# Merge stage regrouped into two seven-product blocks beside three chunks each, with X+Z on VectorE and whole attention outputs in DRAM

## The chip, the cores and the metric

The kernel runs on one core of a Trainium2 chip, in fp32 throughout. The metric is the device time of one execution in microseconds. Before the change the median of three runs is 2468.08 us (2466.44 to 2469.51). The core's engines are TensorE (matrix products), VectorE, ScalarE, GpSimd (POOL) and SyncE (SP); the last two and ScalarE also issue DMAs.

## The reference

Two layers of a decoder trunk, on 256 positions of width 2048. Each layer normalises x, projects it to ten segments, runs two attentions side by side, gates both, projects each, merges them by sigmoid gates and adds an output projection to x.

```python
h = rms_norm(x, norm_gain)
proj = jnp.einsum('bsd,de->bse', h, w_in)
(da_q, da_k, da_v, da_z, sb_q, sb_k, sb_v, sb_z, gate_a, gate_b) = split_columns(proj)
...
ua = oa.reshape(b, s, DA_WIDTH) * jax.nn.silu(da_z)          # differential attention, 8 heads
ub = stick_breaking_attention(qs, ks, vs) * jax.nn.silu(sb_z) # 16 heads
y = (jax.nn.sigmoid(gate_a) * jnp.einsum('bse,ed->bsd', ua, w_branch_a)
     + jax.nn.sigmoid(gate_b) * jnp.einsum('bse,ed->bsd', ub, w_branch_b))
return x + jnp.einsum('bsd,de->bse', y, w_out)
```

Each of the ten segments, the two branch projections and the output projection is a product of 256 x 2048 by 2048 x 2048. The weights are far larger than the core's memory and are streamed once per layer.

## The kernel before, in words

**Splitting.** Each fp32 operand is split into a high part in TensorE's fast fp32 format and the remainder (`split`, L63: a ScalarE copy to `wh`, L64, and a VectorE subtraction to `wl`, L65). A product is three matmuls, high by high, high by low, low by high (`mm3`, L67 to L71). Weights come by DMA into tiles `raw` of 128 x 1024 (512 KB: two slices of 128 rows by 512 columns), loaded on SyncE's queue (`load_raw`, L86 to L88) into a pool of 11 buffers, and are split as soon as they are there.

**A chunk** (`c_stream`, L102) is 512 output columns for all 256 positions: eight steps, each one raw tile and 2 x 2 x 3 = 12 matmuls of 512 columns, into two banks named `mc` (or `sU` and `sN`, with `alt`). After the last step a function `fin` reads the banks; `gap` adds two empty steps, in which the chunk does nothing.

**A block** (`s_stream`, L127) is two chunks at once by a seven-product scheme of Strassen's kind, on 2 x 2 quarters: on the left positions by depth, on the right depth by the two chunks. The weights' quarters are b11, b21, b12 and b22, four raw tiles each. The left sums `sm` (tiles `smh`, `sml`) are made once per layer. The right sums are made in the raw tiles. `add_dma` (L145 to L147) adds a quarter from DRAM to a raw tile by an accumulating DMA on GpSimd's queue, `add` (L149 to L151) adds one raw tile to another on VectorE. The products, four steps each, every step a split and six matmuls, are in order:

| product | right operand | then | bank |
|---|---|---|---|
| first U | X = b11 | X += b12 by DMA | sU, copied to p1 |
| N | Z = b22 | Z += b12 by DMA | sN |
| Q | X | X += b22 by DMA | sQ, copied to p5 (L190) |
| second U | X | | sU, on top; w = U - p5 on VectorE (L195), results with N |
| V | Z | | sQ |
| R | W = b21 | X += W on VectorE (L209) | sN, result with p1 |
| last V | X | | sQ, on top, result with u |

X's four raw tiles are held for the whole block, Z's from N to V.

**The interleave.** `run` (L222) advances several streams by their share of steps done: with weights n, always the stream with the smallest (steps done + 0.5) / n. A block counts 28 steps and a chunk 10 with its gap. So program order mixes block steps and chunk steps; a scheduler then orders each engine's instructions by that order, with weight splits and right sums ahead by a priority offset.

**Stages of a layer.** Differential attention in four groups, all by chunks (L683 to L695); each group's output goes through `da_out` (L577), which transposes it on TensorE, splits it and spills both parts to DRAM by GpSimd DMAs (`spill`, L495). Then four stick-breaking groups (L707 to L733): scores (`sb_weights`), then the block for V and Z beside two chunks, the next group's Q and K; in the fourth group the two chunks are gates a0 and a1. `sb_out` (L626) multiplies, splits and spills. The merge (L778 to L789): a0 and a1 beside the block of gates a2 and a3; a2 and a3 beside the block of gates b0 and b1; then all of ub is reloaded (L782) by GpSimd DMAs, the block of gates b2 and b3 takes nine steps alone, and its rest runs beside b0 (L783 to L786); b1 to b3 follow as plain chunks, and the output projection as four more. `reload` (L699) puts the parts of a group into the tiles listed in `GZ_TAGS`; ub's tiles are those that ua held. Sigmoids of gates and the a-branch products go to DRAM (`sig_d`, `ya_d`) and come back by SyncE (`back`, L738).

**The start.** `first_input` (L333) loads x transposed in pieces of two slices, makes the high part on ScalarE (L339) and the low on VectorE (L340), ahead of the first chunk's weights step by step.

Of the kernel before, what the change touches and what calls it, by code (L numbers as in the profile page):

```python
# [9 lines left out]
F32 = mybir.dt.float32  # L10
# [23 lines left out]
RAW = 11  # L34
# [7 lines left out]
def trunk(ctx: ExitStack, tc: tile.TileContext, x, xT, gT, norm_gain, w_in, qk_gain, lam_vecs,  # L42
# [42 lines left out]

    def load_raw(src):  # L86
        raw = raw_tile()
        nc.sync.dma_start(out=raw, in_=src)  # L88
        return raw
# [7 lines left out]

    def at_k(x, k):

        return x[k // 4][:, k % 4] if isinstance(x, list) else x[:, k]  # L100

    def c_stream(src, lhs, fin, alt=False, gap=0, before=None):  # L102
# [5 lines left out]
        for kp in range(KP):  # L108
            if before is not None:
                before(kp)  # L110
            h, l = split_raw(load_raw(src[kp]))
            order = [(kk, t) for kk in range(KK) for t in range(NT)]
            if kp == KP - 1:
                order.sort(key=lambda o: o[1])
            for kk, t in order:
# [3 lines left out]
                    k == 0, k == KT - 1)  # L119
            if kp < KP - 1:  # L120
                yield
# [5 lines left out]
    def s_stream(sl, sr, xh, sm, fin):  # L127
# [45 lines left out]
        def held(nm):  # L173
            return wp.tile([P, CW], F32, name="pp", bufs=PPB)

# [14 lines left out]
        nc.scalar.copy(p5, q_ps)  # L190
        yield

# [12 lines left out]
        yield  # L205
# [118 lines left out]
    ident = const.tile([P, P], F32, name="ident")  # L324
    make_identity(nc, ident)
    mhalf = const.tile([P, 4], F32, name="mhalf")
    nc.gpsimd.memset(mhalf, -0.5)

# [4 lines left out]
    def first_input(kp):  # L333
        raw = tok()
        nc.sync.dma_start(out=raw, in_=xT[:, kp * CW:(kp + 1) * CW])
        for j in range(KK):
            k = kp * KK + j
            rv = raw[:, j * S:(j + 1) * S]
            nc.scalar.mul(xr[0][:, k], rv, gcol[:, k:k + 1])  # L339
# [5 lines left out]
    def sums_of_squares():  # L345
        for c in range(NG):
            for t in range(NT):
# [6 lines left out]
                     before=first_input)))  # L354
# [15 lines left out]
    for l in range(DEPTH):  # L370
# [42 lines left out]
        u_dram = {b: [dram.tile([P, KT, S], F32R, name=f"u{b}{p}") for p in "hl"] for b in "ab"}  # L413
# [3 lines left out]
        def da_fin(nm, g):  # L417

            def fin(ps):
# [4 lines left out]
                for t in range(NT):  # L424
                    ns.append(work.tile([P, CW], F32, name="ev", bufs=2))
# [65 lines left out]
        def u_stage():  # L491
# [85 lines left out]
        def da_out(g, aT, v, gz):  # L577
# [19 lines left out]
            us = u_stage()  # L597
            for t in range(NT):
                u = tok()
                nc.vector.tensor_tensor(out=u, in0=hold[:, t], in1=gz[:, t], op=ALU.mult)  # L600
                put_T(u, us, 0, t)
# [24 lines left out]
        def sb_out(g, wT, v, gzT):  # L626
            us = u_stage()
            for hp in range(0, HPG, 2):
# [10 lines left out]
                u = tok()  # L639
                uv = u.rearrange("p (h q) -> p h q", q=S)  # L640
                nc.vector.tensor_tensor(out=uv, in0=ov, in1=gzT[:, hp:hp + 2], op=ALU.mult)
                split(us[0][:, hp:hp + 2], us[1][:, hp:hp + 2], uv)
# [63 lines left out]
        ua, ub = ([], []), ([], [])  # L706
        for g in range(NG):  # L707
# [7 lines left out]
            def z_T():  # L715
                gzT.append(att.tile([P, HPG, S], F32, name="gzT", tag="hold"))
                for t in range(NT):
                    tr = ps_at.tile([P, CW], F32, name="at")
                    for h in range(HPG):
# [6 lines left out]
                         lambda col, t, op: (fv, fz)[col](t, op))  # L726
            if g + 1 < NG:
                c = chain(q_stream(NG + g + 1, xt, False, GAP), k_stream(NG + g + 1, xt, False, GAP))
# [153 lines left out]
```

## Time and profile before

| | |
|---|---|
| median of the runs | 2468.08 us |
| the profiled execution's own time | 2464.42 us |
| its span, first to last instruction | 2462.7 us |
| TensorE's mean granted clock | 0.988 |
| TensorE, VectorE, ScalarE, GpSimd busy | 97%, 71%, 62%, 16% |
| moved by DMA | 571.21 MB |

In a table by stretches, each engine has its busy microseconds and (x) its number of instructions in the stretch; then come the granted clock of TensorE (1.00 is full), the mean busy share of the 16 DMA engines, and GB/s. A matmul's recorded time overlaps with the next one's, so that a run of them is read from their starts or their count, and not from durations. A row of waits has who waited for whom, the sum of microseconds, how often, and the longest. A row of groups has, behind the names and shapes, the count, then the busy sum and the mean in ns, then the idle time of the engine ahead of it with what ended that. A row of the timeline has start, duration, engine, line and names, and in brackets the idle time before it. A row of DMAs ends with the size and the median time from issue to landing.

### The profile page before, as it was taken

Reading aid. Unit: us, or ns where it says so; the run is one execution under the profiler, and the core shown is the slowest. Engines: PE = TensorE matmul, PEld = TensorE weight load, DVE = VectorE, ACT = ScalarE, POOL = GpSimd, SP = SyncE. Lnnn points to the kernel's source line nnn. Section 1 sums busy time; section 2 is a strip of 40 time slices with the busy share of each in tenths; the row PEclk is TensorE's granted clock in tenths of the full one; section 3 lists DMA queues with packets and bytes.
Section 4 is the critical chain, followed back from the end, with each engine's and each line's share of the span. In section 5 each row is a group of like instructions: output and inputs, shape, how many; then the busy total and the mean of one; then the engine's idle time right before and its main releaser. Section 6 shows DMA issues by size and latency. Waiting matters only on the chain.

```text
span 2462.7 us, 31649 instructions
## 1 busy us (share of the span) xinstructions
PE 2384.9 (97%) x10996; PEld 1965.0 (80%) x10996; DVE 1743.6 (71%) x1979; ACT 1531.9 (62%) x2214; POOL 393.7 (16%) x476
## 2 busy tenths in 40 slices
PE   8999999999999999899999999999999998997999
PEld 6888888788887777688888888887888877876887
DVE  5677767688787676575666776777887876766754
ACT  6666666677777555454565676667777775655543
POOL 1132230200101211200020321302101112112000
PEclk9999999999999999899999999999999999999999
DMA  9546646888988989987665465378889889899873
GB/s 338 174 141 225 197 137 232 210 239 229 247 239 246 296 266 274 293 315 250 212 207 180 151 221 187 119 249 208 247 238 229 247 248 295 281 289 264 320 233 102
DMA packets 163040, 571.21 MB, mean 232 GB/s; under 512 B 18624, under 2 KB 19136, under 8 KB 162880
## 3 DMA queue, kind: packets, MB, share of 16 engines
q1 hardware_dynamic: 120960, 423.55, 50.8%
q0 software_dynamic: 39328, 141.58, 24.9%
q10 hardware_dynamic: 2592, 4.07, 0.5%
q8 instruction: 86, 1.41, 0.2%
q14 instruction: 74, 0.61, 0.1%
HBM read 535.57 MB, written 33.55 MB: 231 GB/s over the span
## 4 chain that ended last, share of the span: by engine, by line
PE 67%; issue 17%; DMA 7%; POOL 4%; DVE 2%; ACT 2%; POOLq 0%; SPq 0%; ACTq 0%; DVEq 0%
PE mc L69 11%; PE mc L70 11%; PE mc L71 11%; DMA raw<-in_w_in 6%; PE sU L70 4%; PE sN L70 4%; PE sU L71 4%; PE sN L71 4%; PE sN L69 4%; PE sU L69 4%; POOL raw L147 2%; PE at L243 2%; PE sQ L70 1%; PE sQ L69 1%; PE sQ L71 1%
## 5 line engine op out<-in xcount | busy, mean ns | idle before, releaser
L65 DVE TENSOR_TENSOR wl<-raw,wh 128x1024 fp32r<-128x1024 f32 x1000 | 1209.8, 1222 | 495.3 <-PE mc L70 158.9
L64 ACT CAST wh<-raw 128x1024 fp32r<-128x1024 f32 x1000 | 1045.9, 1053 | 724.4 <-PE mc L71 280.9
L147 POOL DMA_DIRECT2D raw<-in_w_in x168 | 145.5, 868 | 743.0 <-DVE wl L65 466.3
L70 PE MATMUL mc<-wl,xTh 128*128 128x512 f32 x576 | 225.9, 392 | 0.4 <-DVE wl L65 0.2
L71 PE MATMUL mc<-wh,xTl 128*128 128x512 f32 x576 | 225.0, 391 | 0.0
L69 PE MATMUL mc<-wh,xTh 128*128 128x512 f32 x576 | 207.0, 394 | 5.5 <-ACT tok L465 3.4
L69 PE MATMUL mc<-wh,xrh 128*128 128x512 f32 x512 | 198.6, 392 | 8.6 <-ACT wh L64 8.5
L70 PE MATMUL mc<-wl,xrh 128*128 128x512 f32 x512 | 201.8, 394 | 1.8 <-DVE wl L65 1.8
L71 PE MATMUL mc<-wh,xrl 128*128 128x512 f32 x512 | 200.9, 392 | 0.0
L69 PEld LDWEIGHTS mc<-wh,xTh 128*128 128x128 f32 x576 | 107.8, 189 | 29.9 <-ACT wh L64 4.3
L70 PEld LDWEIGHTS mc<-wl,xTh 128*128 128x128 f32 x576 | 108.5, 188 | 25.6 <-DVE wl L65 3.5
L71 PEld LDWEIGHTS mc<-wh,xTl 128*128 128x128 f32 x576 | 108.5, 188 | 21.7
L69 PEld LDWEIGHTS mc<-wh,xrh 128*128 128x128 f32 x512 | 96.4, 189 | 29.3 <-ACT wh L64 9.5
L70 PEld LDWEIGHTS mc<-wl,xrh 128*128 128x128 f32 x512 | 96.6, 189 | 23.3 <-DVE wl L65 3.7
L71 PEld LDWEIGHTS mc<-wh,xrl 128*128 128x128 f32 x512 | 96.6, 189 | 19.2
L252 POOL TENSOR_SCALAR rv<-ssq 128x4 f32<-128x4 f32 (+1 forms) x48 | 40.2, 837 | 419.4 <-ACT junk L433 379.4
L70 PE MATMUL sU<-wl,xrh 128*128 128x512 f32 x256 | 100.6, 393 | 1.1 <-DVE wl L65 1.1
L71 PE MATMUL sN<-wh,xrl 128*128 128x512 f32 x256 | 100.5, 393 | 0.0
L70 PE MATMUL mc<-wl,ua 128*128 128x512 f32 x256 | 100.2, 391 | 0.2 <-DVE wl L65 0.2
L71 PE MATMUL sU<-wh,xrl 128*128 128x512 f32 x256 | 100.2, 391 | 0.0
L69 PE MATMUL sN<-wh,xrh 128*128 128x512 f32 x256 | 100.1, 391 | 0.0
L70 PE MATMUL sN<-wl,xrh 128*128 128x512 f32 x256 | 99.9, 390 | 0.0
(258 smaller groups left out, 5010.6 us busy)
## 6 DMA issues: line engine op xcount, KB each, us to landing
raw<-in_w_in SPq DMA_DIRECT2D x584, 512.0 KB, 4.4
raw<-in_w_in POOLq DMA_DIRECT2D x168, 512.0 KB, 9.7
raw<-in_w_a SPq DMA_DIRECT2D x64, 512.0 KB, 5.7
raw<-in_w_b SPq DMA_DIRECT2D x64, 512.0 KB, 5.8
raw<-in_w_o SPq DMA_DIRECT2D x64, 512.0 KB, 4.3
uah<-uh POOLq DMA_DIRECT2D x8, 512.0 KB, 4.9
ual<-ul POOLq DMA_DIRECT2D x8, 512.0 KB, 6.9
ubh<-uh POOLq DMA_DIRECT2D x8, 512.0 KB, 6.4
```

Source lines behind the costliest of these rows:

```text
L64: nc.scalar.copy(h, src)
L65: nc.vector.tensor_tensor(out=l, in0=src, in1=h.bitcast(F32), op=ALU.subtract)
L69: nc.tensor.matmul(ps, lhsT=lh, rhs=rh, start=start, stop=False, **kw)
L70: nc.tensor.matmul(ps, lhsT=lh, rhs=rl, start=False, stop=False, **kw)
L71: nc.tensor.matmul(ps, lhsT=ll, rhs=rh, start=False, stop=stop, **kw)
L147: nc.gpsimd.dma_start(out=dst, in_=src, accum_op=ALU.add)
L243: nc.tensor.transpose(out=tr[:, j * P:(j + 1) * P], in_=src[:, j * P:(j + 1) * P], identity=ident)
L252: nc.gpsimd.tensor_scalar(out=v[:, :w], in0=ss, scalar1=1.0 / n, scalar2=RMS_EPS, op0=ALU.mult, op1=ALU.add)
```

## The change

Blocks get a switch `tb_dma`. With it (stick-breaking groups one to three), Z takes b12 after N and X takes b22 after Q, both by DMA as before, but V comes between Q and the second U. Without it (group four and the merge's blocks), Z stays b22 through N; after each of Q's steps VectorE adds Z to X, and Z then takes b12 by DMA; V stays behind U.

Group four runs its block beside three chunks (gates a0, a1 and b0). The merge has two blocks: gates a2 and a3 beside a0, a1 and the chunk of gate b1; gates b2 and b3 beside a2, a3, the reload of ub and b0. Gates b0 and b1 are so two chunks instead of a block. The attention outputs are spilled as one fp32 tile, loaded back through SyncE's queue into raw tiles and split then. The last stick-breaking group is neither spilled nor reloaded, and the b-branch chunks take its depth first. The raw pool has 12 buffers; the two `ev` buffers are taken from the pool of `pp`. At the start the first weights come and are split in two halves, the first piece of x comes in two, and its high part is made on VectorE. A first copy of two constants, made twice before, goes.

```diff
-RAW = 11
+RAW = 12
...
+    def first_slice(src, between):
+        raw = raw_tile()
+        h = wp.tile([P, KK * CW], F32R, name="wh", bufs=4)
+        l = wp.tile([P, KK * CW], F32R, name="wl")
+        for i in range(KK):
+            c = slice(i * CW, (i + 1) * CW)
+            nc.sync.dma_start(out=raw[:, c], in_=src[:, c])
+            if i == 0:
+                between()
+            with tc.high_priority(offset=400):
+                split(h[:, c], l[:, c], raw[:, c])
+        return h, l
...
-        yield from prod(n_ps, s(3), loader(zs, b22), lambda i: add_dma(zs[i], b12[i]))
+        yield from prod(n_ps, s(3), loader(zs, b22),
+                        (lambda i: add_dma(zs[i], b12[i])) if tb_dma else None)
         yield
+        def next_sums(i):
+            if tb_dma:
+                add_dma(xs[i], b22[i])
+            else:
+                add(xs[i], zs[i])
+                add_dma(zs[i], b12[i])
         q_ps = ps_s.tile([P, CW], F32, name="sQ")
-        yield from prod(q_ps, s(0), lambda i: xs[i], lambda i: add_dma(xs[i], b22[i]))
+        yield from prod(q_ps, s(0), lambda i: xs[i], next_sums)
         p5 = held("p5")
         nc.scalar.copy(p5, q_ps)
         yield
+        if tb_dma:
+            v_ps = ps_s.tile([P, CW], F32, name="sQ")
+            yield from prod(v_ps, s(2), lambda i: zs[i], None, False)
+            yield
         yield from prod(u_ps, s(1), lambda i: xs[i], None, True)
...
-        v_ps = ps_s.tile([P, CW], F32, name="sQ")
-        yield from prod(v_ps, s(2), lambda i: zs[i], None, False)
+        if not tb_dma:
+            v_ps = ps_s.tile([P, CW], F32, name="sQ")
+            yield from prod(v_ps, s(2), lambda i: zs[i], None, False)
...
+            else:
+                nc.sync.dma_start(out=rv, in_=xT[:, k * S:(k + 1) * S])
+                nc.vector.tensor_scalar(out=xr[0][:, k], in0=rv, scalar1=gcol[:, k:k + 1],
+                                        scalar2=None, op0=ALU.mult)
...
-                    ns.append(work.tile([P, CW], F32, name="ev", bufs=2))
+                    ns.append(held("ev"))
...
         def spill(b, g, u):
-            for i in range(2):
-                nc.gpsimd.dma_start(out=u_dram[b][i][:, g * 4:(g + 1) * 4], in_=u[i])
+            nc.gpsimd.dma_start(out=u_dram[b][:, g * 4:(g + 1) * 4], in_=u)
...
         def reload(b, groups, u):
             for g in groups:
+                raw = load_raw(u_dram[b][:, g * 4:(g + 1) * 4].rearrange("p h s -> p (h s)"))
+                ts = [att.tile([P, 4, S], F32R, name="u" + b, tag=tag) for tag in GZ_TAGS[g]]
+                split(ts[0], ts[1], raw.rearrange("p (h s) -> p h s", s=S))
                 for i in range(2):
-                    ut = att.tile([P, 4, S], F32R, name="u" + b, tag=GZ_TAGS[g][i])
-                    nc.gpsimd.dma_start(out=ut, in_=u_dram[b][i][:, g * 4:(g + 1) * 4])
-                    u[i].append(ut)
+                    u[i][g] = ts[i]
...
-                c = chain(c_stream(w_chunk(GATE_A, 0), xt, sig_fin("a", 0), False, GAP),
-                          c_stream(w_chunk(GATE_A, 1), xt, sig_fin("a", 1), False, GAP))
-            run((2 * (C_STEPS + GAP), c), (S_STEPS, s))
-            sb_out(g, wT, v, gzT[0])
+                c = [gate_chunk("a", 0), gate_chunk("a", 1), gate_chunk("b", 0)]
+            run((len(c) * (C_STEPS + GAP), chain(*c)), (S_STEPS, s))
+            last_u = sb_out(g, wT, v, gzT[0])
...
-            return c_stream([w_b[l, c, kp] for kp in range(KP)], ub, fin, alt, gap, before)
+            return c_stream([w_b[l, c, kp] for kp in range(KP)], ub, fin, alt, gap, before,
+                            depth=[KP - 2, KP - 1, *range(KP - 2)])
...
-        run((2 * (C_STEPS + GAP), chain(a_stream(0, False, GAP), a_stream(1, False, GAP))),
-            (S_STEPS, gate_block("a", 2)))
-        run((2 * (C_STEPS + GAP), chain(a_stream(2, False, GAP), a_stream(3, False, GAP))),
-            (S_STEPS, gate_block("b", 0)))
-        reload("b", range(NG), ub)
-        late = gate_block("b", 2)
-        for _ in range(S_STEPS // 3):
-            next(late)
-        run((C_STEPS + GAP, b_stream(0, False, GAP)), (S_STEPS - S_STEPS // 3, late))
+        def back_ub():
+            reload("b", range(NG - 1), ub)
+            yield
+        c = [a_stream(0, False, GAP), a_stream(1, False, GAP), gate_chunk("b", 1)]
+        run((len(c) * (C_STEPS + GAP), chain(*c)), (S_STEPS, gate_block("a", 2)))
+        c = [a_stream(2, False, GAP), a_stream(3, False, GAP), back_ub(), b_stream(0, False, GAP)]
+        run((3 * (C_STEPS + GAP), chain(*c)), (S_STEPS, gate_block("b", 2)))
         run((1, b_stream(1)))
```

More of the change, by code (lines that the diff above doesn't have):

```diff
@@ L84, in raw_tile, with held @@
         return wp.tile([P, KK * CW], F32, name="raw", bufs=RAW)
+    def held(nm):
+        return wp.tile([P, CW], F32, name="pp", bufs=PPB)
     def load_raw(src):
@@ L96, in split_raw, with c_stream @@
         return h, l
+    def first_slice(src, between):
[10 more added lines that the diff above has]
+        return h, l
     def at_k(x, k):
         return x[k // 4][:, k % 4] if isinstance(x, list) else x[:, k]
-    def c_stream(src, lhs, fin, alt=False, gap=0, before=None):
+    def c_stream(src, lhs, fin, alt=False, gap=0, before=None, first=False, depth=range(KP)):
         if alt:
@@ L107, in c_stream @@
             ps = [ps_c.tile([P, CW], F32, name="mc") for _ in range(NT)]
[L108 to L111, printed above, removed]
+        for i, kp in enumerate(depth):
+            if first and i == 0:
+                h, l = first_slice(src[kp], lambda: before(0))
+            else:
+                if before is not None:
+                    before(i)
+                h, l = split_raw(load_raw(src[kp]))
             order = [(kk, t) for kk in range(KK) for t in range(NT)]
-            if kp == KP - 1:
+            if i == KP - 1:
                 order.sort(key=lambda o: o[1])
@@ L118, in c_stream @@
                 mm3(ps[t], at_k(lhs[0], k)[:, ts], at_k(lhs[1], k)[:, ts], h[:, cs], l[:, cs],
-                    k == 0, k == KT - 1)
-            if kp < KP - 1:
+                    i + kk == 0, i == KP - 1 and kk == KK - 1)
+            if i < KP - 1:
                 yield
@@ L125, in c_stream, with s_stream @@
             yield
-    def s_stream(sl, sr, xh, sm, fin):
+    def s_stream(sl, sr, xh, sm, fin, tb_dma=False):
         hk = KP // 2
@@ L199, in s_stream @@
         yield
-        v_ps = ps_s.tile([P, CW], F32, name="sQ")
-        yield from prod(v_ps, s(2), lambda i: zs[i], None, False)
+        if not tb_dma:
+            v_ps = ps_s.tile([P, CW], F32, name="sQ")
+            yield from prod(v_ps, s(2), lambda i: zs[i], None, False)
         fin(1, 1, lambda dst: nc.vector.scalar_tensor_tensor(
             out=dst, in0=v_ps, scalar=-1.0, in1=w, op0=ALU.mult, op1=ALU.subtract))
-        yield
+        if not tb_dma:
+            yield
         def add_w(i):
@@ L334, in first_input @@
         raw = tok()
-        nc.sync.dma_start(out=raw, in_=xT[:, kp * CW:(kp + 1) * CW])
+        if kp:
+            nc.sync.dma_start(out=raw, in_=xT[:, kp * CW:(kp + 1) * CW])
         for j in range(KK):
@@ L338, in first_input @@
             rv = raw[:, j * S:(j + 1) * S]
-            nc.scalar.mul(xr[0][:, k], rv, gcol[:, k:k + 1])
+            if kp:
+                nc.scalar.mul(xr[0][:, k], rv, gcol[:, k:k + 1])
+            else:
+                nc.sync.dma_start(out=rv, in_=xT[:, k * S:(k + 1) * S])
+                nc.vector.tensor_scalar(out=xr[0][:, k], in0=rv, scalar1=gcol[:, k:k + 1],
+                                        scalar2=None, op0=ALU.mult)
             nc.vector.scalar_tensor_tensor(out=xr[1][:, k], in0=rv, scalar=gcol[:, k:k + 1],
@@ L353, in trunk @@
     run((1, c_stream([w_in[0, DA_Q, kp] for kp in range(KP)], xr, lambda ps: first.update(ps=ps),
-                     before=first_input)))
+                     before=first_input, first=True)))
     sums_of_squares()
@@ L600, in da_out @@
                 nc.vector.tensor_tensor(out=u, in0=hold[:, t], in1=gz[:, t], op=ALU.mult)
-                put_T(u, us, 0, t)
+                tr = ps_at.tile([P, CW], F32, name="at")
+                for j in range(HPG):
+                    nc.tensor.transpose(out=tr[:, j * P:(j + 1) * P], in_=u[:, j * P:(j + 1) * P],
+                                        identity=ident)
+                nc.scalar.copy(us[:, :, t * P:(t + 1) * P], heads(tr))
             spill("a", g, us)
@@ L626, in sb_out @@
         def sb_out(g, wT, v, gzT):
-            us = u_stage()
+            keep = g == NG - 1
+            if keep:
+                uh, ul = u_parts()
+            else:
+                us = att.tile([P, HPG, S], F32, name="us", tag="aTh")
             for hp in range(0, HPG, 2):
@@ L638, in sb_out @@
                         False, True)
[L639 to L642, printed above, removed]
+                hs = slice(hp, hp + 2)
+                uv = tok().rearrange("p (h q) -> p h q", q=S) if keep else us[:, hs]
+                nc.vector.tensor_tensor(out=uv, in0=ov, in1=gzT[:, hs], op=ALU.mult)
+                if keep:
+                    split(uh[:, hs], ul[:, hs], uv)
+            if keep:
+                return uh, ul
             spill("b", g, us)
```

24 lines of the change are left out of this document (12 added, 12 removed).

## The prediction, made blind

> **What bounds the kernel now.** I read the page's first part, then busy time by stretches cut at the stages, TensorE's waits, and the timeline around the longest wait.
>
> ```profile
> span 2462.7 us, 31649 instructions
> PE 2384.9 (97%) x10996; PEld 1965.0 (80%) x10996; DVE 1743.6 (71%) x1979; ACT 1531.9 (62%) x2214; POOL 393.7 (16%) x476
> ```
> ```profile
> core 0: us, PE busy (x) PEld busy (x) DVE busy (x) ACT busy (x) POOL busy (x), PEclk, DMA share, GB/s
> 0.00:60.00 60.00, 49.54 (x202) 38.81 (x203) 33.07 (x47) 39.67 (x76) 7.38 (x22) 1.00 0.90 339
> 60.00:466.00 406.00, 405.44 (x1941) 338.62 (x1940) 290.64 (x395) 265.60 (x514) 91.59 (x90) 1.00 0.58 187
> 466.00:745.00 279.00, 275.17 (x1324) 227.85 (x1324) 226.54 (x245) 201.41 (x248) 33.95 (x42) 1.00 0.86 235
> 745.00:1065.00 320.00, 294.15 (x1253) 237.59 (x1252) 219.94 (x206) 186.99 (x201) 57.73 (x81) 0.94 0.94 277
> 1065.00:1690.00 625.00, 624.43 (x2937) 519.73 (x2936) 427.37 (x539) 379.22 (x658) 107.66 (x114) 1.00 0.64 207
> 1690.00:1965.00 275.00, 271.68 (x1311) 225.42 (x1310) 222.07 (x242) 198.10 (x245) 32.51 (x40) 1.00 0.86 237
> 1965.00:2285.00 320.00, 291.42 (x1261) 234.48 (x1260) 220.84 (x208) 188.14 (x202) 58.31 (x82) 0.96 0.94 277
> 2285.00:2463.00 178.00, 173.10 (x778) 142.49 (x776) 103.18 (x104) 72.76 (x75) 4.53 (x7) 1.00 0.63 212
> ```
> TensorE is the bound, and where it idles is plain. Through 60–466 and 1065–1690 (differential attention, then output and the next layer) it idles 0.6 us each. In the first three stick-breaking groups it idles 3.8 and 3.3 us by layer. In the fourth group and the merge it idles 25.9 and 28.6 us, and there the clock is below 1. Per layer that clock is worth 0.06 × 320 = 19.2 and 0.04 × 320 = 12.8 us. Idle and clock in these four stretches make 61.6 + 32.0 = **93.6 us**; all else is matmul at full pace, except the start.
>
> ```profile
> 2390.00:2430.00 40.00, 40.00 (x178) 33.11 (x177) 20.96 (x19) 15.86 (x15) 0.00 (x0) 1.00 0.63 197
> ```
> This stretch holds only 512-column matmuls of the output projection. They overlap, so their price is the spacing: 40 / 178 = 0.225, or 0.227 without the two that straddle the edges. A block step (6 matmuls) takes 1.36 us, a chunk step (12) 2.72 us.
>
> ```profile
> PE sU L69 <- ACT wh L64: 44.0, 11, 9.7
> PE mc L69 <- ACT wh L64: 11.9, 11, 7.5
> PE sU L70 <- DVE wl L65: 6.2, 12, 0.8
> PE mc L69 <- ACT tok L465: 3.4, 2, 1.7
> PE sQ L69 <- ACT wh L64: 2.9, 2, 1.5
> ```
> ```profile
> 859.33 0.39 PE L69 MATMUL sQ<-wh,smh 128*128 128x512 f32 x1
> 866.89 0.79 PE L69 MATMUL sU<-wh,smh 128*128 128x512 f32 x1 [7.17 <-ACT wh L64]
> 867.48 0.63 PE L70 MATMUL sQ<-wl,smh 128*128 128x512 f32 x1
> 867.91 0.63 PE L71 MATMUL sQ<-wh,sml 128*128 128x512 f32 x1
> ...
> 871.32 0.63 PE L71 MATMUL sU<-wh,sml 128*128 128x512 f32 x1
> ```
> ```profile
> 865.79 1.05 ACT L64 CAST wh<-raw 128x1024 fp32r<-128x1024 f32 x1 [10.64 <-DMA raw<-in_w_in]
> ```
> ```profile
> L147 POOL DMA_DIRECT2D raw<-in_w_in x168: 841/861/1152, 435.2 to 2247.4; - x168
>   ACT wh L64: 115.8, 45
> DMA to landing us min/median/max: 5.1/9.7/20.9
> ```
> So nearly all idle time precedes one product: U's second half (sU from the left sums), straight after Q. Its operand is X with b22 added by the accumulating DMA, issued when Q has read X; ScalarE waited for such landings 115.8 us in all. I worked out the interleave of `run` by hand: from Q's first step to U's first lie four block steps and only two chunk steps, because the chunk is then in its two empty steps: 4 × 1.36 + 2 × 2.72 = 10.9 us. A landing takes 9.7 us at the median and 20.9 at worst. That decides it. After the stop the matmuls come 0.43 us apart (867.48 to 867.91), about half pace, until 871.32 and a little on: some 5 us, of which 5 × (1 − 0.227 / 0.43) = 2.4 us are lost.
>
> **The change, part by part.**
>
> *Order.* In the three blocks per layer with accumulated Z (`tb_dma`), V now lies between Q and U. By the same rule from Q0 to U0 there are eight block and four chunk steps: 21.8 us, over the worst landing. In the other three (group four, gates a2–3, b2–3) VectorE makes X+Z, so U waits for no DMA; Z takes b12 by DMA after that, and until V come eight block and eight chunk steps: 32.6 us. The Q-to-U wait goes everywhere. Late next would be X's first accumulation, wanted by Q (8 × 1.36 + 6 × 2.72 = 27 us after U's first step), which is unchanged and late only in the block that today starts with nine steps alone; no block starts alone now. So I remove the 93.6 us and add back what is left.
>
> *Matmuls.* Gates b0 and b1 turn from a block (7 × 24 = 168 matmuls) into two chunks (2 × 96 = 192). 24 more per layer: 48 × 0.227 = **+10.9 us**, on the path.
>
> *Traffic.*
> ```profile
> raw<-in_w_in SPq DMA_DIRECT2D x584, 512.0 KB, 4.4
> ua<-uah POOLq DMA_DIRECT2D x8, 512.0 KB, 8.1
> ```
> Per layer the accumulating DMAs fall from 7 × 12 = 84 to 3 × 12 + 3 × 8 = 60, the block-to-chunk swap adds 4 plain loads, spills fall from 16 to 7 and reloads from 16 to 7: 38 transfers of 512 KB fewer. In group four and merge, weights and reloads were 4 × 24 + 7 × 8 + 16 = 168 transfers and become 3 × 20 + 9 × 8 + 7 = 139. At 277 GB/s before, over a stretch about as long, that is some 230 GB/s, what the earlier groups moved (235) with 1% idle. The new reloads go through SP's queue among the weights (4.4 us each) instead of POOL's (8.1); the three of b stand ahead of b0's own weights, but b0 begins with the group that stayed in SBUF.
>
> *VectorE and ScalarE.*
> ```profile
> L65 DVE TENSOR_TENSOR wl<-raw,wh 128x1024 fp32r<-128x1024 f32 x1000 | 1209.8, 1222 | 495.3 <-PE mc L70 158.9
> L64 ACT CAST wh<-raw 128x1024 fp32r<-128x1024 f32 x1000 | 1045.9, 1053 | 724.4 <-PE mc L71 280.9
> L151 DVE TENSOR_TENSOR raw<-raw 128x1024 f32<-128x1024 f32 x56 | 68.5, 1223 | 24.4 <-DMA raw<-in_w_in 24.1
> L190 ACT COPY pp<-sQ 128x512 f32<-128x512 f32 x14 | 8.1, 578 | 1.8 <-PE sQ L71 1.8
> ```
> Per layer the swap drops 12 splits and 4 additions, the reloads add 7 splits, X+Z adds 12 additions: VectorE +3 × 1.22 us, less 14 half-size low parts that the unsplit spills don't need: about nothing. In a three-chunk stage it has 52 splits and 8 additions, 60 × 1.22 = 73 us, plus some 10 of small work, in 3 × 21.8 + 38.1 = 103.5 us: covered on average. During Q it has 2.45 us a step, and two of those steps have no chunk beside them. R does the same today (split and addition in L209) and shows up in no wait, so between 0 and 1.6 us each I take 0.5: 6 × 0.5 = **+3 us**. If the cover were gone, each of the 24 X+Z additions would cost its 1.22, 29 us.
>
> *A new wait.* V uses the bank sQ that Q just filled, with only an empty chunk step between, so its first matmul waits for the copy p5. Queued behind it on TensorE are V's other matmuls and the next chunk's; ScalarE and VectorE, which wait for those to free the split buffers, stop with it. Bounds: 0, if a chunk's matmul is placed between; 0.39 + 0.58 plus one split ahead on ScalarE (1.05), 2.0 us, at most. The nearest row is the wait for L465, 1.7 us, also a bank held by a ScalarE copy, and only in 2 blocks of 14. I take 1.0: 6 × 1.0 = **+6 us**. The L465 waits stay: **+3.4**.
>
> ```profile
> 760.00:780.00 20.00, 16.56 (x57) 12.15 (x56) 11.21 (x12) 18.23 (x21) 5.00 (x8) 0.74 0.90 266
> 953.00:959.00 6.00, 4.74 (x13) 3.50 (x14) 3.05 (x3) 2.13 (x3) 0.57 (x1) 0.72 1.07 223
> ```
> Such waits keep their bare length only if they stay short. The 1.7 us ones above lie in a stretch at 1.00, but 1.3 us idle in 953–959 already goes with 0.72. I count clock only from there on. The Trainium skill ("TensorE: Matmul & The Clock Gate", Part 1) says that the clock halves after an idle window of about 3.4 us; the trace agrees for the 7.2 us wait and not for 953–959, where less idle time was enough. By the rule alone every remaining wait would cost its length.
>
> *Start.*
> ```profile
> 4.87 0.91 ACT L339 ACTIVATE xrh<-tok,gcol 128x256 fp32r<-128x256 f32 x2 [2.86 <-DMA gcol<-in_gT]
> 6.36 1.05 ACT L64 CAST wh<-raw 128x1024 fp32r<-128x1024 f32 x1 [0.59 <-DMA raw<-in_w_in]
> 7.46 1.22 PE L69 MATMUL mc<-wh,xrh 128*128 128x512 f32 x2 [7.46 <-ACT wh L64]
> ```
> Half of the first weights is loaded and split alone, and VectorE makes xr: the split shrinks by about 0.5 us, and the half load lands earlier. But 339 GB/s runs through these 60 us, so an earlier start can run into later loads. Between 0 and −2.5: **−1.2 us**.
>
> Free: the retained group of b, the one-copy spill (its work lies beside 70–90% busy engines that TensorE doesn't wait for), the shared ring for `ev`, the dropped constants, the twelfth raw buffer.
>
> **Sum**: 2462.7 − 93.6 + 10.9 + 3 + 6 + 3.4 − 1.2 = 2391.2 us span. The profiled execution took 2464.42, 1.7 more than its span, and lies 3.7 under the median of the runs: 2391.2 + 1.7 + 3.7 = **2397 us**.
>
> **Rivals.**
>
> *Slower: bandwidth, not order.* The stretches with the waits have DMA share 0.94. If the landings stretch with the engines' load whatever the order, X+Z and V only move the wait to the weights of the three chunks, and the added matmuls remain: 2468 + 10.9 − 1.2 = 2478. It decides if the share stays at 0.94 and Z's accumulation takes over 32 us in the merge. For it: the one long landing, 20.9 us. Against it: 339 GB/s at the start and the 29 transfers fewer. The change then doesn't do what its order is for.
>
> *V behind p5 is dear.* 2.0 us and half pace after it (2.4) in each of six blocks: 6 × 4.4 = 26 instead of 6, 2417. By the skill's rule, waits of 2.0 us keep the clock: 12 instead of 6, 2403.
>
> *The raw ring chokes at b's reload.* Its three raw tiles wait for a3 to free the tiles of ua, beside X's four and Z's last two: 9 of 12 held, 3 left for loads. A stop like today's longest, 9.7 + 2.4 us, in each layer: +24, 2421. Against: b's splits come as soon as a3 has passed each group.
>
> **Chances.** Forecast with its own range of 2380 to 2410: 0.66. Dear V, choked ring, or VectorE short in Q: 0.21, to 2440. Slower by bandwidth: 0.06. About no change, part of each: 0.03. Everything hidden and the start at its best, 2376 to 2380: 0.04. The range, 2378 to 2435, leaves out the last three and the tail. Runs of before spread by 3 us, so 0.2% (5 us) is what can be told: faster 0.91, same 0.03, slower 0.06.
>
> **What would show it.** Right: TensorE's waits for sU gone from 44 to under 8; the clock 0.99 or more in group four and merge; DMA share there near 0.87; x11044 matmuls; 120 accumulating DMAs; first matmul near 6. Wrong: sU or mc still waiting for ScalarE's split behind DMA landings (bandwidth); new waits of sQ for L190's copy over 10 us; a stop near b0; VectorE's split ending TensorE's waits in Q.

## The result, and the profile after

The changed kernel takes 2406.65 us (median of 4 runs, 2406.20 to 2407.71), beside 2467.26 for the kernel before: ratio 0.9756, interval 0.9739 to 0.9773. It is 2.4% faster; the prediction was 2397 us with a range of 2378 to 2435. The experiments below show that this is not the change's own grouping at work: of its two large parts, one alone (the order of the products) gives 2398, and a third arrangement 2386.

The page's first lines:

```profile
span 2404.2 us, 31450 instructions
PE 2373.1 (99%) x11044; PEld 1966.8 (82%) x11044; DVE 1735.8 (72%) x1950; ACT 1508.3 (63%) x2181; POOL 322.0 (13%) x375
```

There are 48 matmuls more, as counted beforehand, in a span that is 58.5 us shorter. The stretches of the stick-breaking groups and the merge (idle of TensorE is the stretch less PE busy):

```profile
core 0: us, PE busy (x) PEld busy (x) DVE busy (x) ACT busy (x) POOL busy (x), PEclk, DMA share, GB/s
466.00:745.00 279.00, 277.62 (x1349) 232.17 (x1348) 226.97 (x244) 203.84 (x249) 30.75 (x37) 1.00 0.85 234
745.00:1050.00 305.00, 296.65 (x1315) 243.35 (x1314) 229.68 (x211) 184.51 (x195) 31.43 (x45) 0.99 0.82 254
1690.00:1950.00 260.00, 259.31 (x1265) 217.18 (x1264) 211.53 (x225) 188.24 (x228) 25.45 (x31) 1.00 0.81 225
1950.00:2230.00 280.00, 274.26 (x1216) 224.53 (x1216) 214.03 (x197) 170.50 (x179) 29.62 (x42) 1.00 0.83 254
```

Idle is 1.4 + 8.4 + 0.7 + 5.7 = 16.2 us where it was 61.6, and the clock, worth 32 us before, is worth 0.01 × 305 = 3. TensorE's waits, the longest in total:

```profile
PE mc L70 <- DVE wl L65: 9.6, 10, 3.7
PE sQ L70 <- DVE wl L65: 7.1, 10, 1.0
PE mc L69 <- DVE xrh L371: 5.3, 1, 5.3
PE mc L69 <- ACT wh L64: 3.5, 5, 2.3
PE sQ L69 <- ACT pp L216: 1.0, 2, 0.5
```

The row that led before, sU with 44.0 us, is gone. ScalarE's waits for landings tell the same; the first row is of the kernel before, the second of the changed one (longest wait at the end of the row):

```profile
ACT wh L64 <- DMA raw<-in_w_in: 127.1, 53, 13.1
```
```profile
ACT wh L64 <- DMA raw<-in_w_in: 15.4, 7, 4.2
```

And the accumulating DMAs themselves land sooner at worst (median 9.7 and worst 20.9 before):

```profile
L167 POOL DMA_DIRECT2D raw<-in_w_in x120: 838/858/1225, 437.3 to 2179.0; - x120
DMA to landing us min/median/max: 5.2/8.0/9.8
```

Where is the rest? The largest single wait that is left lies around b0's first steps. TensorE, SyncE and VectorE there:

```profile
1014.67 0.40 PE L71 MATMUL sQ<-wh,sml 128*128 128x512 f32 x1
1018.72 0.79 PE L70 MATMUL mc<-wl,uh 128*128 128x512 f32 x1 [3.65 <-DVE wl L65]
1019.31 0.63 PE L71 MATMUL mc<-wh,ul 128*128 128x512 f32 x1
1019.74 0.63 PE L70 MATMUL mc<-wl,uh 128*128 128x512 f32 x1
```
```profile
989.67 7.33 SPq L91 DMA_DIRECT2D raw<-ub  x3
997.83 0.33 SPq L91 DMA_DIRECT2D raw<-in_w_b  x1
998.96 0.33 SPq L91 DMA_DIRECT2D raw<-in_w_in  x1
```
```profile
1016.30 1.23 DVE L171 TENSOR_TENSOR raw<-raw 128x1024 f32<-128x1024 f32 x1 [2.72 <-DMA raw<-in_w_in]
```

The three reloads of b hold SyncE's queue for 7 us, and the weights behind them come late. VectorE then stops at an addition of R, whose raw tile has not landed (2.72 us), and the split that TensorE wants stands behind it. Counting each spacing of matmul starts above 0.227 us, some 8 us are lost there in the first layer and 4.5 in the second. The Trainium skill ("TensorE: Matmul & The Clock Gate", Part 1) has the clock halve after an idle window of some 3.4 us; these rows agree, with 3.65 us idle and 0.43 us from start to start behind it. Other stops here do not: half pace also follows 2.25 us idle at this kernel's start (the rows stand under "The start and the ring"). None of the waits around 1 us in this kernel shows it.

The same addition explains the waits of sQ (7.1 us). All ten lie in V, in the blocks that make X+Z on VectorE, and none in Q, where the X+Z additions stand. One of them, VectorE and then TensorE:

```profile
794.51 1.23 DVE L171 TENSOR_TENSOR raw<-raw 128x1024 f32<-128x1024 f32 x1 [2.09 <-DMA raw<-in_w_in]
795.66 3.49 DVE L65 TENSOR_TENSOR wl<-raw,wh 128x1024 fp32r<-128x1024 f32 x3
```
```profile
796.93 0.50 PE L70 MATMUL sQ<-wl,smh 128*128 128x512 f32 x1 [0.71 <-DVE wl L65]
```

U has been read out by then (L225 at 791.02), so that L171 here is R's addition X += W, whose operand has not landed, and V's last split stands behind it. Ahead of six of the ten VectorE stood 0.7 to 2.2 us in this way; the other four are at b0.

### The profile page after: what moved, and what is told of

It is laid out like the page before. It is cut to its first block, busy times and chain, and to the rows that moved or that the text cites. A ratio compares the mean times of both kernels' runs of the same rounds, so it can differ in the third digit from the quotient of the medians.

```text
span 2404.2 us, 31450 instructions
## 1 busy us (share of the span) xinstructions
PE 2373.1 (99%) x11044; PEld 1966.8 (82%) x11044; DVE 1735.8 (72%) x1950; ACT 1508.3 (63%) x2181; POOL 322.0 (13%) x375
## 4 chain that ended last, share of the span: by engine, by line
PE 95%; DMA 2%; DVE 1%; issue 1%; ACT 0%; SPq 0%; DVEq 0%; ACTq 0%
PE mc L70 17%; PE mc L71 16%; PE mc L69 16%; PE sU L70 5%; PE sN L71 5%; PE sU L69 5%; PE sN L70 5%; PE sU L71 5%; PE sN L69 5%; PE sQ L70 3%; PE sQ L69 2%; PE sQ L71 2%; PE at L275 2%; DMA raw<-in_w_in 1%; PE at L70 1%; PE at L71 1%
## 5 line engine op out<-in xcount | busy, mean ns | idle before, releaser
L65 DVE TENSOR_TENSOR wl<-raw,wh 128x1024 fp32r<-128x1024 f32 (+1 forms) x977 | 1184.7, 1223 | 464.1 <-PE mc L70 202.2
L64 ACT CAST wh<-raw 128x1024 fp32r<-128x1024 f32 (+1 forms) x977 | 1022.1, 1051 | 693.2 <-PE mc L71 381.9
L70 PE MATMUL mc<-wl,xTh 128*128 128x512 f32 x704 | 275.2, 391 | 3.3 <-DVE wl L65 3.3
L71 PE MATMUL mc<-wh,xTl 128*128 128x512 f32 x704 | 274.2, 389 | 0.0
L69 PE MATMUL mc<-wh,xTh 128*128 128x512 f32 x704 | 253.2, 391 | 0.2 <-ACT wh L64 0.2
L167 POOL DMA_DIRECT2D raw<-in_w_in x120 | 103.6, 868 | 742.4 <-DVE wl L65 507.5
L70 PEld LDWEIGHTS mc<-wl,xTh 128*128 128x128 f32 x704 | 132.2, 188 | 32.0 <-DVE wl L65 5.3
L69 PEld LDWEIGHTS mc<-wh,xTh 128*128 128x128 f32 x704 | 131.5, 188 | 28.3 <-ACT wh L64 1.2
L71 PEld LDWEIGHTS mc<-wh,xTl 128*128 128x128 f32 x704 | 132.2, 188 | 26.8
L69 PE MATMUL sU<-wh,xrh 128*128 128x512 f32 x256 | 100.0, 391 | 0.0
```

Source lines behind the costliest of these rows:

```text
L64: nc.scalar.copy(h, src)
L65: nc.vector.tensor_tensor(out=l, in0=src, in1=h.bitcast(F32), op=ALU.subtract)
L69: nc.tensor.matmul(ps, lhsT=lh, rhs=rh, start=start, stop=False, **kw)
L70: nc.tensor.matmul(ps, lhsT=lh, rhs=rl, start=False, stop=False, **kw)
L71: nc.tensor.matmul(ps, lhsT=ll, rhs=rh, start=False, stop=stop, **kw)
L167: nc.gpsimd.dma_start(out=dst, in_=src, accum_op=ALU.add)
```

## The experiments

Times are medians, and each edit starts from the changed kernel. The kernel before, run beside them, took 2465.2 to 2467.7 us in the four sittings.

**The order alone undone, the grouping alone undone, both undone.** These three close a square with the changed kernel. The old order:

```diff
-                        (lambda i: add_dma(zs[i], b12[i])) if tb_dma else None)
+                        lambda i: add_dma(zs[i], b12[i]))
...
-            if tb_dma:
-                add_dma(xs[i], b22[i])
-            else:
-                add(xs[i], zs[i])
-                add_dma(zs[i], b12[i])
+            add_dma(xs[i], b22[i])
...
-        if tb_dma:
-            v_ps = ps_s.tile([P, CW], F32, name="sQ")
-            yield from prod(v_ps, s(2), lambda i: zs[i], None, False)
-            yield
...
```

> The changed kernel with the products' order and sums of before in every block (Z takes b12 after N and X takes b22 after Q, both by DMA, and U follows Q); grouping, spills and start stay changed. Theory A (order): U waits for X's accumulation again; in the six blocks of the first three groups as before, 3.5 us idle a layer, and in the other six with three chunks beside them, where Q to U lasts 13.6 us by the interleave and not 10.9, some 1 to 3 us each: 2420 us, at least 2414, with the waits of sU for ScalarE's split back at 10 to 25 us. Rival (bandwidth: the waits of before came from the load on the DMA engines, which the new grouping removes): within 3 us of the changed kernel, 2407.

The old grouping:

```diff
-                c = [gate_chunk("a", 0), gate_chunk("a", 1), gate_chunk("b", 0)]
+                c = [gate_chunk("a", 0), gate_chunk("a", 1)]
...
-        c = [a_stream(0, False, GAP), a_stream(1, False, GAP), gate_chunk("b", 1)]
+        c = [a_stream(0, False, GAP), a_stream(1, False, GAP)]
         run((len(c) * (C_STEPS + GAP), chain(*c)), (S_STEPS, gate_block("a", 2)))
-        c = [a_stream(2, False, GAP), a_stream(3, False, GAP), back_ub(), b_stream(0, False, GAP)]
-        run((3 * (C_STEPS + GAP), chain(*c)), (S_STEPS, gate_block("b", 2)))
+        c = [a_stream(2, False, GAP), a_stream(3, False, GAP)]
+        run((len(c) * (C_STEPS + GAP), chain(*c)), (S_STEPS, gate_block("b", 0)))
+        reload("b", range(NG - 1), ub)
+        late = gate_block("b", 2)
+        for _ in range(S_STEPS // 3):
+            next(late)
+        run((C_STEPS + GAP, b_stream(0, False, GAP)), (S_STEPS - S_STEPS // 3, late))
...
```

> The changed kernel with the grouping of before: two chunks beside the block of group four and of each merge block, gates b0 and b1 as a block, the block of gates b2 and b3 alone for nine steps and then beside b0. Order, sums, spills and start stay changed; 48 matmuls fewer (10.9 us). Theory A (order does most, but the block that starts alone keeps loading at the DMA engines' limit): waits of about 13 us a layer with their clock remain around that block, those of the other blocks go: 2406.65 - 10.9 + 2 x 10 = 2416 us. Rival (bandwidth: at two chunks a block the load is too high whatever the order): 2440 us or more. Third (order alone does it all): 2396 us, and the new grouping was not needed.

Both of these edits together:

> The changed kernel with both the grouping and the order of before; what stays of the change is the unsplit spill, the kept last group of b, twelve raw buffers, the shared ring for ev, and the start. With the runs of the old order alone (2414.6) and the old grouping alone (2398.2) it closes a square. Theory A (order and grouping are two cures of one wait, Q to U, and the rest is worth little): the waits of sU come back, 30 to 44 us, and the time is 2450 to 2465 us. Rival (much of the gain came from the rest, above all from 38 transfers a layer fewer): 2425 to 2440 us.

| us | order before | order changed |
|---|---|---|
| grouping before | 2456.83 | 2398.19 |
| grouping changed | 2414.60 | 2406.65 |

With the old grouping the new order is worth 58.6 us, with the new one 8.0. The new grouping is worth 42.2 us under the old order, and costs 8.5 under the new. The four were timed in three sittings; by the ratios to the kernel before (0.9966, 0.9718, 0.9781 and 0.9756) the two small entries are 6 and 9 us, and only the intervals behind the second, 0.9702 to 0.9733 and 0.9739 to 0.9773, don't overlap. They are two cures of one wait: the order puts work between Q and U, or takes the DMA out; a third chunk puts chunk steps where the gap was. The waits confirm it. With both undone sU waits again as before:

```profile
PE sU L69 <- ACT wh L64: 34.6, 9, 9.9
PE mc L69 <- ACT wh L64: 6.3, 9, 2.5
```

and ScalarE waits for landings 124.4 us there, 64.2 with the old order alone, 26.0 with the old grouping alone, 15.4 in the changed kernel:

```profile
ACT wh L64 <- DMA raw<-in_w_in: 124.4, 48, 10.7
```
```profile
ACT wh L64 <- DMA raw<-in_w_in: 64.2, 36, 4.3
```
```profile
ACT wh L64 <- DMA raw<-in_w_in: 26.0, 14, 4.5
```

For the old order alone the time (2414.6) was what was expected at the least (2414), but the waits of sU were not: 1.8 us instead of 10 to 25. What differs from the run with both undone is the way from Q to U, 13.6 us instead of 10.9, and not the load: in 745 to 1050 us the DMA share is 0.91 in both, and an accumulating DMA lands after 8.5 and 8.7 us at the median, 16.7 and 20.3 at worst. So the longer way is the likely reason; no run varied it alone. The loss that is left is spread. For the old grouping the third expectation, that order does it all (2396), is the nearest. What the block that starts alone still loses stands in the last 50 us of its merge:

```profile
745.00:1050.00 305.00, 298.02 (x1317) 244.31 (x1316) 258.30 (x243) 198.02 (x211) 38.28 (x53) 0.99 0.88 264
975.00:1025.00 50.00, 45.29 (x183) 36.09 (x182) 39.22 (x37) 29.40 (x32) 10.51 (x15) 0.93 0.93 257
```

4.7 us of the 7.0 idle lie there, with the clock at 0.93. All the other edits of the change together (both undone, against the kernel before on that chip): ratio 0.9966, interval 0.9954 to 0.9979, 8 us.

**The reload of b one group at a time.**

```diff
+            def before(i):
+                back_sy(i)
+                if late is not None and i % 2 == 0 and i // 2 < NG - 1:
+                    late(i // 2)
...
-        c = [a_stream(2, False, GAP), a_stream(3, False, GAP), back_ub(), b_stream(0, False, GAP)]
+        c = [a_stream(2, False, GAP), a_stream(3, False, GAP),
+             b_stream(0, False, GAP, lambda g: reload("b", [g], ub))]
```

> The changed kernel, with b's three groups reloaded one by one beside b0's first, third and fifth step, and no longer all three behind a3. Lost around b0's first steps in the changed kernel are about 8 us in the first layer and 4.5 in the second (its longest wait, 3.7 us and the half clock behind it, is there). Theory A (the three reload tiles fill the raw ring and the weights behind them on SyncE's queue come late): that loss goes to about 3 in both layers together, 2397 us. Rival (it is VectorE, which has the splits of the reload, X's additions and the ends of two chunks to do in the same 15 us): the work remains, 2404 to 2407 us.

2401.28 us (2399.03 to 2405.96), 5.4 less; the intervals of the two ratios overlap (0.9714 to 0.9751 here), so the reading rests on the trace. The stretches around b0, first the changed kernel, then this one:

```profile
995.00:1025.00 30.00, 24.34 (x97) 18.49 (x96) 24.70 (x24) 15.67 (x18) 3.23 (x6) 0.94 0.81 273
2190.00:2220.00 30.00, 26.88 (x114) 20.74 (x114) 26.40 (x26) 18.01 (x20) 2.23 (x4) 1.00 0.81 264
```
```profile
995.00:1025.00 30.00, 28.06 (x120) 21.81 (x119) 23.23 (x23) 17.60 (x19) 3.28 (x6) 1.00 0.77 280
2190.00:2220.00 30.00, 28.35 (x121) 22.15 (x121) 25.53 (x26) 17.51 (x19) 2.22 (x4) 1.00 0.82 285
```

VectorE's work in the 30 us is about the same (24.7 and 23.2; 26.4 and 25.5), and idle falls from 5.7 and 3.1 us to 1.9 and 1.7. So it is when the loads come, as theory A had it, and not VectorE's work (that the ring of raw tiles is full there, as the theory also said, these rows don't show); of the gain it foresaw a little over half came.

**The attention outputs split before the spill, as before.**

```diff
-            nc.gpsimd.dma_start(out=u_dram[b][:, g * 4:(g + 1) * 4], in_=u)
+            for i in range(2):
+                nc.gpsimd.dma_start(out=u_dram[b][i][:, g * 4:(g + 1) * 4], in_=u[i])
...
-                raw = load_raw(u_dram[b][:, g * 4:(g + 1) * 4].rearrange("p h s -> p (h s)"))
...
-                split(ts[0], ts[1], raw.rearrange("p (h s) -> p h s", s=S))
                 for i in range(2):
+                    nc.gpsimd.dma_start(out=ts[i], in_=u_dram[b][i][:, g * 4:(g + 1) * 4])
```

> The changed kernel with the attention outputs split before the spill, as before: two DMAs of 512 KB for each group out and two in, all on GpSimd's queue, no raw tiles and no splits for the reload. The last group of b stays kept, order and grouping stay changed. 9 + 9 minus 7 + 7, that is 14 transfers a layer more, 7 splits fewer in the merge. Theory A (the loss at b0 comes from reload tiles in the raw ring): the loss around b0's first steps, about 8 and 4 us, goes and nothing comes back elsewhere: 2397 us. Rival (the unsplit spill is needed, since the load on the DMA engines would else delay loads and sums): 2412 us or more. The prediction counted it as free: 2406.65 within 3.

2424.81 us, 18 slower. Around b0 the loss fell to some 3 and 4 us, as theory A said, but more came back elsewhere. The rival had the wrong reason: ScalarE waits for landings no longer than in the changed kernel.

```profile
ACT wh L64 <- DMA raw<-in_w_in: 14.0, 6, 4.3
```

What stops TensorE is the order on ScalarE. One of four such places, TensorE and then ScalarE:

```profile
584.28 0.74 PE L69 MATMUL mc<-wh,xTh 128*128 128x512 f32 x2 [1.79 <-ACT wh L64]
```
```profile
578.24 0.63 ACT L644 ACTIVATE tok<-tok 128x512 f32<-128x512 f32 x1 [0.34 <-DVE tok L514]
578.78 0.62 ACT L648 ACTIVATE tok<-tok 128x512 f32<-128x512 f32 x1
579.30 0.58 ACT L498 ACTIVATE tok<-mc 128x512 f32<-128x512 f32 x1
579.77 0.62 ACT L645 ACTIVATE tok<-tok 128x512 f32<-128x512 f32 x1
580.30 1.04 ACT L64 CAST wh<-raw 128x1024 fp32r<-128x1024 f32 x1
581.23 0.60 ACT L498 ACTIVATE tok<-mc 128x512 f32<-128x512 f32 x1
581.72 0.63 ACT L646 ACTIVATE tok<-tok 128x512 f32<-128x512 f32 x1
582.24 1.98 ACT L64 CAST wh<-raw 128x1024 fp32r<-128x1024 f32 x2
```

Six activations, four of them of the next group's stick-breaking weights (L644 to L648), surround a single weight split; the two that TensorE is waiting for come at 582.24. Behind each of the four places the matmuls come at half pace for 3.4 us, here after 1.79 us idle. The split outputs occupy two tiles until their DMAs are done, aTh and aTl, which the next group's weights need; the unsplit output occupies one. That this is why that work falls later is argued, not tried. The reloads' landings cost some more, with two waits of `mc` for ua's high parts and two for its low parts, 1.6 us each in sum.

**V first in every block, no X+Z.**

```diff
-    def s_stream(sl, sr, xh, sm, fin, tb_dma=False):
+    def s_stream(sl, sr, xh, sm, fin, _tb=False):
+        tb_dma = True
```

> The changed kernel with all blocks in the order of the first three groups: Z and X take b12 and b22 by DMA, V between Q and U; no X+Z on VectorE anywhere. 24 accumulating DMAs more in all, 24 additions of 1.22 us on VectorE fewer. Theory A (VectorE is what TensorE waits for in Q, 7.1 us before sQ's second matmuls, and the order alone keeps the landings off the path): those waits go, 2400 us. Rival (beside three chunks the DMA load is too high for the accumulations): waits of ScalarE's split behind landings, 2415 us or more. Third (X+Z on VectorE is neutral): 2406.65 within 3.

2403.81 us (2402.99 to 2405.09), 2.8 below the changed kernel. Beside the kernel before the two can't be told apart (0.9752, interval 0.9738 to 0.9767, and 0.9756): beside three chunks X+Z on VectorE buys nothing, and that it costs something isn't shown. The wait of sQ for VectorE's split (7.1) is gone, and some came back at b's reload. Theory A's reason, VectorE short in Q, doesn't hold, since those waits lay in V; this order puts U between V and R, and so no addition of R ahead of V's last split.

**Two chunks beside each of seven blocks.** The square and the reload suggest it: the new order, no added matmuls, no block that runs alone, since gates b0 and b1 are ready before the last block and b0 and b1 can run beside it.

```diff
-                c = [gate_chunk("a", 0), gate_chunk("a", 1), gate_chunk("b", 0)]
+                c = [gate_chunk("a", 0), gate_chunk("a", 1)]
...
-        c = [a_stream(0, False, GAP), a_stream(1, False, GAP), gate_chunk("b", 1)]
+        c = [a_stream(0, False, GAP), a_stream(1, False, GAP)]
         run((len(c) * (C_STEPS + GAP), chain(*c)), (S_STEPS, gate_block("a", 2)))
-        c = [a_stream(2, False, GAP), a_stream(3, False, GAP), back_ub(), b_stream(0, False, GAP)]
-        run((3 * (C_STEPS + GAP), chain(*c)), (S_STEPS, gate_block("b", 2)))
-        run((1, b_stream(1)))
+        c = [a_stream(2, False, GAP), a_stream(3, False, GAP)]
+        run((len(c) * (C_STEPS + GAP), chain(*c)), (S_STEPS, gate_block("b", 0)))
+        c = [b_stream(0, False, GAP, lambda g: reload("b", [g], ub)), b_stream(1, False, GAP)]
+        run((len(c) * (C_STEPS + GAP), chain(*c)), (S_STEPS, gate_block("b", 2)))
...
```

> The changed kernel with seven blocks a layer and two chunks beside each: gates a0 and a1 in group four, then a0 and a1 beside gates a2-3, a2 and a3 beside gates b0-1, b0 and b1 beside gates b2-3, with b's groups reloaded one by one in b0. No block ever runs alone, and the 48 matmuls (10.9 us) are saved. Theory A (order cures the wait; the grouping is worth only what the block that starts alone loses, some 16 us in both layers of the run with the old grouping, and the reload some 5): 2398.2 - 10 = 2388 us, at most 2392. Rival (three blocks in a row with two chunks load the DMA engines too much): 2398 us or more.

2385.95 us (2385.20 to 2388.90), ratio to the kernel before 0.9682, interval 0.9667 to 0.9696, and 20.7 us under the changed kernel. The same with V first everywhere:

> Two chunks beside each of seven blocks, b's reload spread (2385.95), now with V first and all sums by DMA in every block, no X+Z on VectorE: 32 additions of 1.22 us fewer, 32 accumulating DMAs more. Theory A (beside three chunks X+Z cost 3 us against V first, 2406.65 against 2403.81, and the DMA load leaves room): 2383 us. Rival (with two chunks beside each block the load is higher than there, and X+Z saves the landings from being late): 2389 us or more, with waits for sums by DMA in the merge.

2417.63 us, 31.7 slower than with X+Z. The merge of the two, with X+Z first:

```profile
745.00:1050.00 305.00, 301.84 (x1349) 247.74 (x1348) 257.14 (x242) 196.43 (x209) 37.60 (x52) 1.00 0.89 265
```
```profile
745.00:1050.00 305.00, 292.39 (x1284) 239.70 (x1284) 229.47 (x214) 187.77 (x200) 48.49 (x64) 0.98 0.95 280
```
```profile
ACT wh L64 <- DMA raw<-in_w_b: 25.0, 7, 11.4
ACT wh L64 <- DMA raw<-in_w_in: 24.3, 9, 5.4
```

Here the rival of the prediction, load on the DMA engines, holds: the share is back at 0.95. But it is plain weights of the b chunks that come late (25.0 us in 7 waits; the longest b load lands 25.2 us after its issue, 15.3 with X+Z), and no wait of sU is among TensorE's. So X+Z pays where the load is high. That it does so by the 32 transfers that it saves is read from the share and the landings; the run moves V as well. Some of the loss is also order on ScalarE, where a score activation (L659) comes late behind two table loads and weight splits:

```profile
PE at L537 <- ACT tok L659: 9.5, 2, 5.0
```

**The start and the ring.** The old start in the changed kernel:

```diff
-                nc.vector.tensor_scalar(out=xr[0][:, k], in0=rv, scalar1=gcol[:, k:k + 1],
-                                        scalar2=None, op0=ALU.mult)
+            nc.scalar.mul(xr[0][:, k], rv, gcol[:, k:k + 1])
...
-                     before=first_input, first=True)))
+                     before=first_input)))
```

> The changed kernel with the start of before: the first weights in one load of 512 KB, the first piece of x in one, its high part on ScalarE. In the changed kernel the first matmul starts 2.2 us earlier (5.30 against 7.46) but the 193rd 2.6 us later (60.42 against 57.84). Theory A (the loads at the start run at the DMA engines' pace, and the finer start only puts them in a worse order): first matmul at 7.5, 193rd near 57.8, time 2404 us, 2.6 below the changed kernel's 2406.65. Theory B (the delay is chance of the one execution, and the early start gains what the prediction gave it): 2407.9 us, 1.2 above.

Eleven raw buffers in the changed kernel (`RAW = 11`):

> The changed kernel with eleven raw buffers instead of twelve. Two questions. At the start, the 193rd matmul came at 57.84 before, 60.42 in the changed kernel and 59.84 with the old start back, so 2 us of the delay are not the finer start's. Theory A (the twelfth buffer lets the weights run further ahead of the loads of x at the start): 193rd matmul at 58.4. At b0, theory A of the ring: one buffer fewer makes the loss there grow from 8 and 4 us to 10 to 16 in sum over 12. Sum: 2406.65 - 2 + 2 to 8 = 2407 to 2413 us. Rival (the count of buffers matters nowhere): 60.4 and 2406.65 within 2.

The first 60 us: changed kernel, old start, eleven buffers (the kernel before had 202 matmuls there):

```profile
0.00:60.00 60.00, 49.91 (x191) 37.83 (x192) 29.83 (x41) 34.47 (x61) 3.90 (x15) 0.97 0.91 340
```
```profile
0.00:60.00 60.00, 48.87 (x193) 38.17 (x194) 30.75 (x44) 36.92 (x69) 4.77 (x15) 0.97 0.91 342
```
```profile
0.00:60.00 60.00, 49.99 (x195) 37.15 (x196) 30.79 (x45) 36.84 (x69) 4.70 (x15) 1.00 0.90 335
```

The changed kernel starts at 5.30 and not 7.46 us, and is 11 matmuls behind by 60 us: 2.5 us. The old start gives 2405.90 and two matmuls back, eleven buffers 2403.40 and four; as ratios, 0.9748 and 0.9754 beside 0.9756, neither time can be told from the changed kernel's. So neither the finer start nor the buffer explains the delay alone. The clock is a part of it: the changed kernel has 0.97 there and the kernel before 1.00, which is worth 1.8 us. TensorE, behind a split that waited for weights:

```profile
27.34 0.73 PE L69 MATMUL mc<-wh,xrh 128*128 128x512 f32 x2 [2.25 <-ACT wh L64]
29.19 0.63 PE L71 MATMUL mc<-wh,xrl 128*128 128x512 f32 x1
29.62 0.63 PE L70 MATMUL mc<-wl,xrh 128*128 128x512 f32 x1
```

With eleven buffers the clock stays at 1.00, and 7 of the 11 matmuls are missing all the same. For the ring at b0 my theory had the sign wrong: with eleven buffers the loss there fell (to 2.9 and 3.5 us), while the first three groups of the first layer lost more (1331 matmuls from 466 to 745 us instead of 1349, some 4 us). In the two-chunk kernel the old start changes nothing, and then one buffer fewer a great deal:

> Two chunks beside each of seven blocks, b's reload spread (2385.95), now with the start of before. Theory A (the finer start costs 0.7 us, as in the run with the old start): 2385 us, 193rd matmul 0.6 us earlier than 60.17. Rival (chance): no difference, 2386 within 0.5.

2385.74 us, within the runs' spread of 2385.95.

> Two chunks beside each of seven blocks, b's reload spread, the old start (2385.74), now with eleven raw buffers. In the changed kernel one buffer fewer gave 3.2 us (2403.40 against 2406.65), mostly around b0, where the loss fell from 8.4 and 4.5 us to 2.9 and 3.5, against what the ring theory had it do. Theory A (the gain there was the placing of b's reload, which is gone here; at the start the 193rd matmul comes near 58.5 instead of 59.94): 2384 us. Rival (the twelfth buffer is needed where the load is highest, beside two chunks): 2390 us or more. A best version, if A holds.

2404.61 us, 18.9 slower. ScalarE waits for weights longer, 34.1 us in 19 waits instead of 11.5 in 7 with twelve buffers, but that alone isn't the cause: in the changed kernel with eleven it is 32.0 in 22, and the time is no worse. The first three groups lose as much as there (1333 matmuls from 466 to 745 us instead of 1349); what is added is a loss in the merge (1326 instead of 1350 from 745 to 1050), where the changed kernel gained at b0. Why stays open.

```profile
ACT wh L64 <- DMA raw<-in_w_in: 34.1, 19, 5.0
```

## Why the prediction was right, point by point

- **The wait and its cause** (order, 93.6 us to be removed): right. The idle and clock of the four stretches fell to 16.2 + 3 = 19 us, of which I had put back 12.4. The square shows that the order suffices for it. What the prediction did not see is that the grouping cures the same wait again, so that its price is not paid for by anything: my sum was of the whole change and gave no term to the grouping but its matmuls.
- **Matmuls, +10.9**: right by count; undoing the grouping gained 8.5 us of it.
- **V behind p5, +6**: too high. The row for L216 has 1.0 us in 2 waits, so the lower bound of 0 was the nearer; the rival that made it dear is out.
- **VectorE in Q, +3**: nothing of it came in Q. sQ waited 7.1 us for VectorE's split, in 10 waits of at most 1.0, but all in V, behind R's additions; the prediction had no term for that.
- **The L465 waits, +3.4**: gone; no such row is among TensorE's waits.
- **The raw ring at b's reload**: the rival came true in part. I gave it 12 us a layer; it took some 8 and 4.5. The place was right (spreading the reload gained 5.4 us); that the ring is what chokes isn't shown (with eleven buffers the loss there was smaller). It was also one of the signs named for being wrong, a stop near b0.
- **Start, −1.2**: wrong in sign. The first matmul comes 2.2 us earlier, and after 60 us the kernel is 2.5 us behind. It is the one case that the bounds, 0 to −2.5, left out; 1.8 us go with the clock of 0.97.
- **Free edits**: the unsplit spill is worth 18 us beside this grouping. My step counted transfers and busy time and found nothing; what the trace shows without it is TensorE stopped by the order of ScalarE's work. With the split spill kept, the sum would have been the same 2397 and the time 2424.81: that the spill was among the edits is luck for the forecast.
- **Clock**: the 1.3 us of 953–959 are only the window's part of a stop of 2.44 us. Half pace follows waits that short in the changed kernel too (2.25 us at the start), so the price of 2403 for a dear V, in which waits of 2.0 us keep the clock, isn't borne out.
- **Sum**: 2391.2 us span predicted, 2404.2 measured. 6.8 of the 13 are the remaining waits (19.2 against 12.4), 3.7 the start (+2.5 against −1.2), and 2.5 are within the rounding of the clock, which at 0.01 of 305 us is 3. The closeness is partly luck: of the 12.4 us put back for waits 1.0 came where they were put (L216), and most of the rest is at b0 and in V.
- **Bandwidth, the slower rival**: wrong for this kernel, with a share of 0.82 to 0.83 in the merge (though it moved 254 GB/s there and not the 230 of my step on traffic). At 0.95, in the two-chunk kernel without X+Z, the weights do come late.

## What to carry to other kernels

When one wait governs, two edits that both remove it don't add up: price each with the other already there, or the one that costs matmuls looks useful when it isn't. Write down the steps between the issue of a transfer and its first use, at the very places where a neighbouring stream pauses, and compare that with the worst landing. An edit that costs no busy time can still move the order on an engine in front of the bound, so a "free" spill or reload wants its own run.

## What the runs showed of the hardware that was not expected

The order with X+Z on VectorE, beside V first with all sums by DMA, makes no difference that can be told beside three chunks (DMA share 0.82 instead of 0.91 in 745 to 1050 us) and saves 31.7 us beside two (0.89 instead of 0.95). Between the last two shares ScalarE's wait for the b chunks' plain loads goes from 7.1 to 25.0 us, while the worst accumulating landing is 17 us in both two-chunk kernels. One raw buffer of twelve makes no difference that can be told in one schedule and costs 18.9 us in another; why stays open, as does the part of the delay at the start that is left where the clock is full (7 matmuls with eleven buffers, 1.6 us). Half pace followed 1.79, 2.25 and 3.65 us of idle TensorE alike.
